# Where a second query projection stands in the opening of an encoder-layer kernel, and the order of its loads

## The chip, the cores and the metric

The kernel runs on one core of one Trainium2 chip. The metric is the device time of one execution in microseconds (us); a comparison uses the median of several runs. TensorE is PE in the profile (PEld its weight loads), VectorE is DVE, ScalarE is ACT, GpSimd is POOL, and SP is the engine that here only issues transfers. An "SPq" row is a transfer being issued by SP.

## The reference

One layer of a bidirectional encoder, on 1024 tokens of width 1024, in float32. The part that the change touches is the beginning:

```
mod = silu(c) @ w_ada + b_ada;  sh1, sc1, ... = split(mod, 6)
h   = rms_norm(x, norm_mix_g) * (1 + sc1) + sh1
q_a, k_a, v_a, qk_m, v_m, o_m, gates = split(h @ w_in)
y_attn = axial_gqa_attention(rope(rms_norm(q_a)), rope(rms_norm(k_a)), v_a)   # 8 heads, 2 kv heads
y_mem  = bidirectional_mlstm(silu(conv(qk_m)), v_m, o_m, gates)               # 4 heads
x = x + g1 * (concat(y_attn, y_mem) @ w_out)
... then the same norm and modulation, a SwiGLU feed-forward, a last norm
```

Two facts about it matter. The norm's root is one number per token and sc1, norm_mix_g are one number per channel, so h = (x * gain) * root + sh1, with gain = norm_mix_g * (1 + sc1). And so h @ w = ((x * gain) @ w) * root + sh1 @ w: a projection can be made on the *scaled* input z = x * gain before the root is known, and be mended afterwards with the root (per token) and with the shift row sh1 @ w (per output channel).

## The kernel before

Channels lie on the 128 partitions (eight tiles k of x, each 128 x 1024 tokens) and tokens along them, in two halves n of 512. To keep float32 accuracy, every operand of a matmul is split into a high part (a rounding to the PE's format, on ACT) and a low part (the rest, on DVE or POOL), and a product is three matmuls, `mm3` (L311): high by high, low by high, high by low. `hh`, `hl` are the two parts of the input, `whi`, `wlo` those of a weight piece (256 KB, from a raw buffer `wst`, of which there are three; six buffers for the split ones).

The whole program is laid out at build time by a small clock, `Clock` (L127): chains of steps are run in the order in which a model of the engines' durations says that they become ready, and instructions are emitted in that order. The engines then run in the order so written, each in sequence, and wait on semaphores. SP's queue is such a sequence too: a transfer whose buffer isn't free holds all that stand behind it.

The opening goes like this.
- `loads` (L590) lists the first transfers: `x0` to `x7`, `a8` to `a15` (rows of w_ada for the gain), `w` (raw weight pieces), then `a0` to `a7` (rows for the shift). Modulation rows (`ada`) are 512 KB and use five buffers; the dot with silu(c) on DVE frees each.
- For every k, `z_steps` makes the split scaled input from x and the gain, `square_steps` the squares for the norm. TensorE runs, for each k, three first units on it (key pair, value pair, first query unit, in `acc0`), for both halves: 18 matmuls of 512 columns for each k. After k = 5 the sums of squares are closed (L720) and `rstd_steps` makes the root. At k = 3 three `load_piece` calls split the next pieces; a piece's raw transfer is issued only when its own `load_piece` comes.
- `h_steps` (L686) then makes the normalized input in the same buffers as the scaled one: DVE multiplies x by the root, ACT applies gain and shift, ACT makes the high part, POOL the low one (DVE for the very first). The DVE step waits until TensorE has read the scaled input of this k (`z_read`).
- Behind that stand, on the normalized input, the chunk unit ("t", 0) (values of the memory heads and the gates, eight token blocks of 272 columns, tag `acct`) and the second query unit ("q", 1): for the first half of the tokens woven into the same loop over k, for the second half after the chunk unit's second half. `chunk_out` evicts each block into a staging buffer `vstg` (three of them) and stores it.
- `shift_sums` (L631) multiplies the shift into the weights that were used on the scaled input (`wagain`, loaded again by `load_again`, three of 512 KB); `rope_steps` and `v_steps` take the accumulators, multiply by the root (`rooted`), add the shift row (`shifted`) and go on with norm and rotation. For the second query unit `rooted` is a plain ACT copy.
- Then units from the list `IN` (third and fourth query, convolutions, chunks) run until the fourth query is rotated and the gates are ready, and attention starts (scores L1159, transposes L1191, values L1210), with the remaining units as filling between its matmuls.

Of the kernel before, what the change touches and what calls it, by code (L numbers as in the profile page):

```python
# [11 lines left out]
F32 = mybir.dt.float32  # L12
# [28 lines left out]
WARM = 34  # L41
PES = 3
# [43 lines left out]
class Engine:  # L86
# [5 lines left out]
    def __getattr__(self, op):  # L92
        fn = getattr(self.eng, op)

        def emit(*args, **kw):
            n = max(math.prod(a.shape[1:]) for a in args if hasattr(a, "shape"))
            self.clock.run(self.name, self.cost(op, n, args, kw))
            return fn(*args, **kw)  # L98
        return emit
# [27 lines left out]
class Clock:  # L127


    def __init__(self):  # L130
        self.t = self.now = self.fin = self.dma_t = self.dma_q = 0.0
        self.q = []
        self.n = 0
        self.free = {"act": 0.0, "dve": 0.0, "gps": 0.0}
        self.table = "exp"
        self.tick = None

    def run(self, eng, cost):
        e = self.free[eng] = max(self.free[eng], self.now) + cost
# [110 lines left out]
def layer_kernel(ctx, tc, xT, c, w_ada, vecs, cons, rope, w_f, w_fT, w_t0, w_t, w_o, w_gu, w_d, out):  # L250
# [114 lines left out]
    with tc.manual_schedule():  # L365
# [63 lines left out]
        start = {("t", 0): [6, 8, 9, 11], ("q", 1): [7, 10]}  # L429
        t0, q1 = chunk_w(0), conv_w(3)  # L430
        specs += [t0[0], q1[0], t0[1], t0[2], q1[1], t0[3]]
# [56 lines left out]
        def load_piece():  # L488
# [4 lines left out]
            while len(made) <= min(i + (AHEAD if i + AHEAD >= start["down"] else 0), len(specs) - 1):  # L493
# [3 lines left out]
            if isinstance(specs[i][0], str):  # L497
# [3 lines left out]
                  lo=dve if i >= start["down"] or i < 9 or start["o", 0] <= i < start["b", 1] else None)  # L501
# [21 lines left out]
        masks = stp.tile([P, 2 * P], F32, name="masks")  # L523
        nc.scalar.dma_start(masks, cons[:, P + 138:])
# [8 lines left out]
        sh2 = stp.tile([P, 3, 2], F32, name="sh2")  # L533
        shift = stp.tile([P, 3], F32, name="shift")
        shiftg = stp.tile([P, 3], F32, name="shiftg")
# [50 lines left out]
        for k in range(KT):  # L586
# [4 lines left out]
                 "x6", "x7", "a14", "a15", "a0", "a1", "a2", "a3", "a4", "a5", "a6", "a7"]  # L591

        def issue():
# [5 lines left out]
            elif kind == "a":  # L599
                ada_load(i)  # L600
            else:
# [29 lines left out]
        def shift_sums():  # L631
# [9 lines left out]
            def dot(f3, i):  # L641
                w = wagain[f3][:, halves(i)]
                dve.scalar_tensor_tensor(w, w, 1.0, rows[i][0], op0=OP.mult, op1=OP.mult, accum_out=sh2[:, f3, i:i + 1])
                if f3 == 2:
# [5 lines left out]
            def gains():  # L650
                for f3, n in ((0, "k_norm_g"), (2, "q_norm_g")):
# [17 lines left out]
        def load_again():  # L669

            for i in range(3):
# [10 lines left out]
        acc0 = [[psum_tile([P, HALF], "acc") for _ in range(NH)] for _ in range(3)]  # L682
# [17 lines left out]
        for k in range(KT):  # L700
            for n in range(NH):
                ck.need(z_ok[k][n])
                for f in range(3):
# [3 lines left out]
            if k < PES:  # L707
                for n in range(NH):
                    ck.need(sq_ok[k][n])
                    nc.tensor.matmul(msp[n][0], ones, by_pe[k, n], start=k == 0, stop=False)  # L710
                    ck.pe(0.86)
            z_read[k].set(ck, ck.t)
            if k == 3:
                for _ in range(3):
                    load_piece()
            if k == 5:
                for n in range(NH):
# [5 lines left out]
                    y_ok.append(ck.chain(0.0, rstd_ok[n], lambda n=n: act.activation(msp[n][0], rstd[n], AF.Copy)))  # L723
                for n in range(NH):
# [11 lines left out]
        def rope_steps(i, accs, raw=None, qg=None, more=FREE):  # L736
# [18 lines left out]
            def rooted(n):  # L755
                if raw < 0:
                    act.activation(qg[:, halves(n)], accs[n][0], AF.Copy)
                else:
                    dve.tensor_mul(qg[:, halves(n)], accs[n][0], rstd[n])
                accs[n][1].set(ck, ck.fin + LAT)  # L760

            def shifted():
                room()
                act.activation(X["sq"], qg, AF.Square, bias=shift[:, raw:raw + 1] if raw >= 0 else 0.0)
                act.activation(qg, qg, AF.Identity, scale=g, bias=shiftg[:, raw:raw + 1] if raw >= 0 else 0.0)
# [52 lines left out]
            else:  # L818
                ck.chain(0.0, rstd_ok[0], lambda: rooted(0), rstd_ok[1], more, lambda: rooted(1), shift_ok,
# [3 lines left out]
        def v_steps(accs):  # L823
            vt = bp.tile([P, S], F32, tag="big", name="vt")
# [98 lines left out]
        def chunk_out(ci, j, acc, f):  # L923
# [3 lines left out]
            stg = bp.tile([P, 2, P], F32, tag="vstg", name="vstg", bufs=3)  # L927
# [1193 lines left out]
        rope_steps(4, acc0[0], 0, raw_q[2])  # L2121
        rope_steps(0, acc0[2], 2, raw_q[0])
        for _ in range(3):
            load_piece()
        ck.chain(0.0, *sh_ok, load_again)
        ck.chain(0.0, y_free, load_tables)
        accs, tiles = [], []
        for n in range(NH):
            for j in range(4):
                ck.need(slot("acct").flag())  # L2130
                tiles.append(psum_tile([P, 272], "acct"))
            if n == 0:
# [209 lines left out]
```

## Time and profile before

| | us |
|---|---|
| runs, median (lowest, highest) of 3 | 1352.85 (1349.62, 1353.93) |
| the profiled execution | 1348.1 |
| its span | 1346.3 |
| PE / DVE / ACT / POOL busy in it | 1275.8 / 1053.4 / 709.6 / 537.6 |
| first matmul on the scaled input, last one | 11.6, 52.1 |
| first matmul on the normalized input | 57.0 |
| first scores of attention | 168.3 |

The profile is of one execution. A row of a timeline gives the start, the duration, the engine, the line, the operation with the tiles it writes and reads, how often, and in brackets how long the engine had stood idle before it and what released it. Every operation of DVE, ACT and POOL bears L98, the helper that emits them, so tiles tell them apart. A row of the busy table gives a stretch, its length, the busy time of PE, PEld, DVE, ACT and POOL with their instructions, the granted TensorE clock (1.00 is full), the DMA share and GB/s.

### The profile page before, as it was taken

The numbers are of one execution on the slowest core, as the hardware profiler recorded it, in microseconds if no ns is written. First come the engines' busy times: TensorE is split into PE (matmuls) and PEld (weight loads), VectorE is DVE, ScalarE is ACT, GpSimd is POOL, SyncE is SP. The second block draws the span as 40 slices with busy tenths as digits, with TensorE's granted clock in tenths as the row PEclk, the third lists the DMA queues.
The fourth block names the chain that finished last, engine by engine and source line by source line (L and its number), as shares of the span: only waits on it lengthen the run. The fifth ranks groups of instructions, "written<-read, shape, count | busy, mean of one in ns | idle before, by whom it ended". The sixth has DMA issues, their size and how long they took to land.

```text
span 1346.3 us, 19691 instructions
## 1 busy us (share of the span) xinstructions
PE 1275.8 (95%) x6656; PEld 1076.8 (80%) x6656; DVE 1053.4 (78%) x1683; ACT 709.6 (53%) x1342; POOL 537.6 (40%) x454
## 2 busy tenths in 40 slices
PE   9898888899999989999999999999999999999997
PEld 7687677888788988788778788888888887788886
DVE  6946699976689847989888989876666656888886
ACT  6575466778577855555477522333332334454462
POOL 0262578655666523444225155554544530000002
PEclk9898999999999999999999999999999999999999
DMA  9454433333233226673553344423332248933314
GB/s 362 139 154 134 115 104 100 86 103 109 67 93 107 74 82 193 218 271 114 181 173 116 108 143 144 138 94 110 111 117 78 80 170 314 340 106 94 94 56 164
DMA packets 104469, 187.04 MB, mean 139 GB/s; under 512 B 11568, under 2 KB 33200, under 8 KB 104368
## 3 DMA queue, kind: packets, MB, share of 16 engines
q1 hardware_dynamic: 90976, 163.68, 37.7%
q10 hardware_dynamic: 13392, 22.10, 4.3%
q8 instruction: 53, 0.87, 0.3%
q14 instruction: 48, 0.39, 0.1%
HBM read 139.33 MB, written 42.73 MB: 135 GB/s over the span
## 4 chain that ended last, share of the span: by engine, by line
PE 62%; DVE 20%; DMA 6%; ACT 5%; issue 4%; POOL 2%; SPq 1%; ACTq 0%; DVEq 0%; POOLq 0%
PE acc L312 17%; PE acc L314 17%; PE acc L313 17%; DVE sst L98 3%; DVE x L98 3%; DVE y L98 3%; DVE PT L98 2%; PE av L1210 2%; PE T L1191 2%; DVE ada L98 1%; PE S L1159 1%; DMA wst<-act_d 1%; ACT P L98 1%; DVE wlo L98 1%; PE ni L2001 1%
## 5 line engine op out<-in xcount | busy, mean ns | idle before, releaser
L98 ACT ACTIVATE whi<-wst 128x512 fp32r<-128x512 f32 (+2 forms) x223 | 134.0, 606 | 145.0 <-PE acc L314 61.0
L98 POOL TENSOR_TENSOR wlo<-wst,whi 128x512 fp32r<-128x512 f32 (+1 forms) x83 | 130.1, 1573 | 174.8 <-ACT whi L98 126.2
L313 PE MATMUL acc<-x,whi 128*128 128x512 f32 x352 | 136.9, 389 | 0.0
L98 POOL TENSOR_SCALAR P<-P,sst 128x1024 f32<-128x1024 f32 x64 | 85.9, 1343 | 85.5 <-DVE sst L98 64.2
L98 DVE TENSOR_TENSOR wlo<-wst,whi 128x512 fp32r<-128x512 f32 (+2 forms) x140 | 92.3, 663 | 30.6 <-ACT whi L98 30.1
L312 PE MATMUL acc<-hh,whi 128*128 128x512 f32 x224 | 96.3, 430 | 8.4 <-ACT xp L98 6.4
L98 POOL TENSOR_TENSOR x<-x,ny 128x256 f32<-128x256 f32 (+1 forms) x8 | 8.3, 1068 | 232.3 <-PE acc L314 212.3
L98 POOL TENSOR_TENSOR wlo<-wr,whi 128x512 fp32r<-128x512 f32 x52 | 72.3, 1389 | 71.5 <-ACT whi L98 68.4
L314 PE MATMUL acc<-whi,wcl 128*128 128x512 f32 x244 | 95.3, 390 | 2.2 <-DVE wcl L98 2.2
L312 PE MATMUL acc<-whi,wch 128*128 128x512 f32 x244 | 95.0, 390 | 1.2 <-ACT wch L98 1.2
L313 PE MATMUL acc<-wlo,wch 128*128 128x512 f32 x244 | 95.0, 389 | 0.0
L98 ACT ACTIVATE P<-S,sst,colq 128x1024 f32<-128x1024 f32 x64 | 77.2, 1206 | 31.9 <-DVE sst L98 26.9
L98 DVE TENSOR_TENSOR PT<-T,PT 128x512 fp32r<-128x512 f32 x128 | 83.4, 681 | 9.4 <-ACT PT L98 9.2
L313 PE MATMUL acc<-hl,whi 128*128 128x512 f32 x224 | 89.6, 400 | 0.3 <-DVE hl L98 0.3
L314 PE MATMUL acc<-hh,wlo 128*128 128x512 f32 x224 | 89.3, 399 | 0.1
L98 ACT ACTIVATE whi<-wr 128x512 fp32r<-128x512 f32 x56 | 35.3, 632 | 99.1 <-DVE wr L98 48.3
L312 PE MATMUL acct<-whi,hh 128*128 128x256 f32 (+1 forms) x256 | 81.4, 318 | 5.8 <-ACT hh L98 4.5
L98 ACT ACTIVATE PT<-T 128x512 fp32r<-128x512 f32 x128 | 71.7, 595 | 27.7 <-PE T L1191 26.9
L98 DVE TENSOR_REDUCE sst<-S 128x1 f32<-128x1024 f32 x64 | 77.6, 1213 | 7.6 <-PE S L1159 7.5
L1191 PE MATMUL T<-ident,P 128*128 128x128 f32 x512 | 71.2, 276 | 12.9 <-DVE PT L98 10.0
L98 POOL TENSOR_TENSOR ada<-ada,cond 128x512 f32<-128x512 f32 x48 | 72.2, 1507 | 20.5 <-DMA ada<-in_w_ada_dram 20.2
L1210 PE MATMUL av<-PT,va 128*128 128x256 f32 x512 | 71.9, 287 | 7.0 <-DVE PT L98 6.8
(482 smaller groups left out, 3851.3 us busy)
## 6 DMA issues: line engine op xcount, KB each, us to landing
wr<-in_w_gu_dram SPq DMA_DIRECT2D x66, 256.0 KB, 2.7
ada<-in_w_ada_dram SPq DMA_DIRECT2D x64, 256.0 KB, 3.4
wd<-in_w_d_dram SPq DMA_DIRECT2D x22, 512.0 KB, 6.6
wst<-in_w_gu_dram SPq DMA_DIRECT2D x42, 256.0 KB, 3.0
wst<-act_d SPq DMA_DIRECT2D x33, 256.0 KB, 3.6
ada<-in_w_ada_dram SPq DMA_DIRECT2D x16, 512.0 KB, 7.4
wst<-in_w_o_dram SPq DMA_DIRECT2D x32, 256.0 KB, 3.2
act_d<-sg ACTq DMA_DIRECT2D x29, 256.0 KB, 2.0
```

The lines of the kernel that those rows point to most:

```text
L98: return fn(*args, **kw)
L312: nc.tensor.matmul(acc, w[0], x[0], start=first, stop=False)
L313: nc.tensor.matmul(acc, w[0], x[1], start=False, stop=False)
L314: nc.tensor.matmul(acc, w[1], x[0], start=False, stop=last)
L1159: nc.tensor.matmul(sp[:, halves(n)], qs[:, j * P:(j + 1) * P], k2[g][m][:, halves(n)], start=m == 0, stop=m == 1)
L1191: nc.tensor.transpose(tp[:, k], Pt[q][:, (4 * b + k) * P:(4 * b + k + 1) * P], ident)
L1210: nc.tensor.matmul(av, va[:, k, h // 4], PT[it][m][:, k], start=(k, m) == (0, 0), stop=(k, m) == (NJ - 1, 1))
L2001: nc.tensor.matmul(ni, x["q"][:, i * P:(i + 1) * P], H["Cs"][b][:, i4], start=True, stop=True)
```

## The change

The second query unit moves from the normalized input to the scaled one and stands ahead of the chunk unit. The third of the first units (first query) is multiplied in two parts: k < `TAIL` in the common loop, the rest behind it. The root's sums are closed inside step k = `SUMS`. The query's correction then needs a fourth shift row. `h_steps` does gain and root in one DVE step, which no longer waits for `z_read`, and only the writing of the parts does; for three steps the parts are made straight from x by ACT and DVE. In `loads`, raw transfers `r` of six pieces stand ahead of and among a0 to a7, and in `load_piece` raw transfers run two pieces ahead for the third and fourth query and the first conv unit. The low parts of pieces 9 to 11 go from POOL to DVE. The masks are loaded at the end of the opening, by SP into another tile, instead of at the start by ACT. The last block of each half of the chunk unit has a staging buffer of its own. The value tile takes the place of the row of squares. The planner's clock now keeps DVE and POOL apart, in its model alone, where both have two inputs in SBUF, until attention starts.

```diff
+TAIL = 4
+SUMS = 6
...
+        if two and self.lock and eng in self.two:
+            other = "gps" if eng == "dve" else "dve"
+            s = max([s] + [b for a, b in self.two[other] if a <= s < b])
+            self.two[eng] = self.two[eng][-7:] + [(s, s + cost)]
...
-        start = {("t", 0): [6, 8, 9, 11], ("q", 1): [7, 10]}
+        start = {("t", 0): [8, 9, 10, 11], ("q", 1): [6, 7]}
...
-            while len(made) <= min(i + (AHEAD if i + AHEAD >= start["down"] else 0), len(specs) - 1):
+            while len(made) <= min(i + (AHEAD if i + AHEAD >= start["down"] or start["q", 2] <= i < start["f", 4] else 0), len(specs) - 1):
...
-                  lo=dve if i >= start["down"] or i < 9 or start["o", 0] <= i < start["b", 1] else None)
+                  lo=dve if i >= start["down"] or i < 12 or start["o", 0] <= i < start["b", 1] else None)
...
-        masks = stp.tile([P, 2 * P], F32, name="masks")
-        nc.scalar.dma_start(masks, cons[:, P + 138:])
...
-                 "x6", "x7", "a14", "a15", "a0", "a1", "a2", "a3", "a4", "a5", "a6", "a7"]
+                 "x6", "x7", "a14", "a15", "r", "r", "r", "a0", "a1", "a2", "a3", "a4", "r", "r", "r", "a5", "a6", "a7"]
...
+            elif kind == "r":
+                piece(len(made))
...
-            dots = [ck.chain(LAT, again[f3], lambda f3=f3: [dot(f3, i) for i in range(2)]) for f3 in range(3)]
+            dots = [ck.chain(LAT, again[f3], h_mul[4 + f3], lambda f3=f3: [dot(f3, i) for i in range(2)]) for f3 in range(4)]
...
+            def scaled():
+                dve.scalar_tensor_tensor(xs, xs, sc1[:, k:k + 1], rstd[n] if k < 2 else msp[n][0],
+                                         op0=OP.mult, op1=OP.mult)
+                if n:
+                    h_mul[k].set(ck, ck.fin)
...
-                0.0, *after, (rstd_ok if k < 2 else y_ok)[n], z_read[k],
-                lambda: dve.tensor_mul(xs, xs, rstd[n] if k < 2 else msp[n][0]), sh_ok[k],
-                lambda: act.activation(xs, xs, AF.Identity, scale=sc1[:, k:k + 1], bias=mod[:, k:k + 1]),
-                lambda: act.activation(h_hi[k][:, halves(n)], xs, AF.Copy),
-                lambda: (gps if n or k else dve).tensor_sub(h_lo[k][:, halves(n)], xs, h_hi[k][:, halves(n)].bitcast(F32)))
+                0.0, *after, (rstd_ok if k < 2 else y_ok)[n],
+                scaled, sh_ok[k], z_read[k],
+                *([lambda: act.activation(h_hi[k][:, halves(n)], xs, AF.Identity, bias=mod[:, k:k + 1]),
+                   lambda: dve.scalar_tensor_tensor(h_lo[k][:, halves(n)], xs, mod[:, k:k + 1],
+                                                    h_hi[k][:, halves(n)].bitcast(F32), op0=OP.add, op1=OP.subtract)]
+                  if n == 0 and k < 3 else
+                  [lambda: act.activation(xs, xs, AF.Identity, bias=mod[:, k:k + 1]),
+                   lambda: act.activation(h_hi[k][:, halves(n)], xs, AF.Copy),
+                   lambda: gps.tensor_sub(h_lo[k][:, halves(n)], xs, h_hi[k][:, halves(n)].bitcast(F32))]))
...
-                for f in range(3):
+                for f in range(3 if k < TAIL else 2):
...
-            stg = bp.tile([P, 2, P], F32, tag="vstg", name="vstg", bufs=3)
+            stg = (stp.tile([P, 2, P], F32, tag="vst0", name="vstg", bufs=1) if ci == 0 and j % 4 == 3 else
+                   bp.tile([P, 2, P], F32, tag="vstg", name="vstg", bufs=3))
...
+        for n in range(NH):
+            for k in range(TAIL, KT):
+                mm3(acc0[2][n][0], weights([2, 5], k, 4), (h_hi[k][:, halves(n)], h_lo[k][:, halves(n)]),
+                    k == 0, k == KT - 1)
+                ck.pe(0.68)
         rope_steps(0, acc0[2], 2, raw_q[0])
...
+        for k in range(KT):
+            for n in range(NH):
+                if k == 0:
+                    ck.need(slot("acc").flag())
+                    accs.append(psum_tile([P, HALF], "acc"))
                 mm3(accs[n][0], weights(start["q", 1], k, 4), (h_hi[k][:, halves(n)], h_lo[k][:, halves(n)]),
                     k == 0, k == KT - 1)
                 ck.pe(0.68)
+            z_read[k].set(ck, ck.t)
+            if k == 1:
+                for _ in range(3):
+                    load_piece()
+        rope_steps(1, accs, 3, raw_q[1])
```

After that the chunk unit stands alone: for each half, k = 0 to 5 over its four blocks, and then k = 6 and 7 block by block, each evicted as it ends; between them six more `load_piece` calls. `shift_sums` follows the first half as before.

More of the change, by code (lines that the diff above doesn't have):

```diff
@@ L96, in emit @@
             n = max(math.prod(a.shape[1:]) for a in args if hasattr(a, "shape"))
-            self.clock.run(self.name, self.cost(op, n, args, kw))
+            ins = [a for a in args[1:] if hasattr(a, "shape") and math.prod(a.shape[1:]) > 8]
+            self.clock.run(self.name, self.cost(op, n, args, kw),
+                           len(ins) == 2 and all(getattr(a, "space", None) != PSUM for a in ins))
             return fn(*args, **kw)
@@ L669, in load_again @@
         def load_again():
-            for i in range(3):
+            for i in range(4):
                 w = wagain[i] = bp.tile([P, S], F32, tag="big", name="wagain")
@@ L680, in load_tables @@
             ck.chain(arrive, lambda: None, flag=rp_ok)
-        acc0 = [[psum_tile([P, HALF], "acc") for _ in range(NH)] for _ in range(3)]
+        acc0 = [[None] * NH for _ in range(3)]
+        for f, n in ((0, 0), (1, 0), (0, 1), (1, 1), (2, 0), (2, 1)):
+            acc0[f][n] = psum_tile([P, HALF], "acc")
+        h_mul = [Flag() for _ in range(KT)]
         for _ in range(WARM):
@@ L706, in layer_kernel @@
                     ck.pe(0.68)
[L707 to L717, printed above, removed]
+                if k == SUMS:
                     ck.need(sq_ok[7][n])
@@ L723, in layer_kernel @@
                     y_ok.append(ck.chain(0.0, rstd_ok[n], lambda n=n: act.activation(msp[n][0], rstd[n], AF.Copy)))
+            if k < PES:
+                for n in range(NH):
+                    ck.need(sq_ok[k][n])
+                    nc.tensor.matmul(msp[n][0], ones, by_pe[k, n], start=k == 0, stop=False)
+                    ck.pe(0.86)
+            if k == 3:
+                for _ in range(3):
+                    load_piece()
+            if k == SUMS:
                 for n in range(NH):
@@ L734, in layer_kernel, with rope_steps @@
         va_ok = [Flag(), Flag()]
-        def rope_steps(i, accs, raw=None, qg=None, more=FREE):
+        def rope_steps(i, accs, raw=None, qg=None):
             is_k = i == 4
@@ L755, in rooted @@
             def rooted(n):
[L756 to L759, printed above, removed]
+                dve.tensor_mul(qg[:, halves(n)], accs[n][0], rstd[n])
                 accs[n][1].set(ck, ck.fin + LAT)
@@ L823, in v_steps @@
         def v_steps(accs):
-            vt = bp.tile([P, S], F32, tag="big", name="vt")
+            vt = ssx_t
             def transpose(b):
@@ L2145, in query, with chunk_step @@
                 ck.pe(0.68)
-            for k in range(KT):
-                ck.need(h_ok[n][k])
-                chunk_step(k)
-                if n == 0:
-                    query(k)
-                elif k % 2:
-                    load_piece()
-            for j in range(4 * n, 4 * n + 4):
-                chunk_out(0, j, *tiles[j])
+            z_read[k].set(ck, ck.t)
+            if k == 1:
+                for _ in range(3):
+                    load_piece()
+        rope_steps(1, accs, 3, raw_q[1])
+        ck.chain(0.0, *sh_ok, load_again)
+        ck.chain(0.0, y_free, load_tables)
+        for n in range(NH):
+            def chunk_step(j, k):
+                ck.need(h_ok[n][k])
+                if k == 0:
+                    ck.need(slot("acct").flag())
+                    tiles.append(psum_tile([P, 272], "acct"))
+                s = slice(j * P, (j + 1) * P)
+                mm3(tiles[j][0], (h_hi[k][:, s], h_lo[k][:, s]), weights(start["t", 0], k, 2), k == 0, k == KT - 1)
+                ck.pe(0.38)
+                if k == KT - 1:
+                    chunk_out(0, j, *tiles[j])
+            js = range(4 * n, 4 * n + 4)
+            for k in range(KT - 2):
+                for j in js:
+                    chunk_step(j, k)
+                if k % 2 and (n or k < 4):
+                    load_piece()
+            for j in js:
+                for k in range(KT - 2, KT):
+                    chunk_step(j, k)
+            if n:
+                load_piece()
             if n == 0:
-                more = Flag()
-                rope_steps(1, accs, -1, raw_q[1], more)
                 while not again:
@@ L2163, in layer_kernel @@
                 ck.chain(0.0, *vo_ok[0], gate_steps)
-                ck.need(slot("acc").flag())
-                accs.append(psum_tile([P, HALF], "acc"))
-                for k in range(KT):
-                    query(k)
-                    if k % 4 == 3:
-                        load_piece()
-                more.set(ck, ck.t)
+        masks = small()
+        maskin = dma(masks[:, 0:2 * P], cons[:, P + 138:])
         for e in range(2):
             for i in range(2):
-                ck.at(1.0, lambda e=e, i=i: dve.tensor_copy(maskb[:, e, i], masks[:, e * P:(e + 1) * P]))
+                ck.at(maskin, lambda e=e, i=i: dve.tensor_copy(maskb[:, e, i], masks[:, e * P:(e + 1) * P]))
         un = Stream(units(IN))
```

46 lines of the change are left out of this document (17 added, 29 removed).

## The prediction

> **What bounds the kernel now.** I read the page first, for the share of each engine, then busy time by stretches of the opening, then TensorE's waits, then the timeline of each engine around the two long ones.
>
> ```profile
> span 1346.3 us, 19691 instructions
> PE 1275.8 (95%) x6656; PEld 1076.8 (80%) x6656; DVE 1053.4 (78%) x1683; ACT 709.6 (53%) x1342; POOL 537.6 (40%) x454
> ```
>
> TensorE is busy 95% of the span, so only 70 us in the whole kernel are not matmul. Where they lie decides. Busy time by stretches (busy microseconds of PE, PEld, DVE, ACT, POOL, then the granted TensorE clock):
>
> ```profile
> 50.00:60.00 10.00, 4.81 (x19) 3.72 (x19) 10.00 (x17) 7.68 (x14) 1.78 (x2) 0.85 0.40 133
> 60.00:70.00 10.00, 8.76 (x49) 8.00 (x48) 10.00 (x13) 5.33 (x10) 10.00 (x6) 0.81 0.28 71
> 100.00:110.00 10.00, 6.24 (x18) 4.04 (x17) 6.10 (x8) 3.70 (x8) 3.49 (x2) 0.73 0.40 123
> 110.00:120.00 10.00, 10.00 (x51) 8.39 (x50) 9.38 (x17) 4.83 (x8) 2.69 (x2) 0.92 0.27 88
> 52.30:111.70 59.40, 47.93 (x273) 41.14 (x273) 38.89 (x67) 40.82 (x76) 33.72 (x23) 0.89 0.39 117
> ```
>
> The last row is the stretch that the change rewrites: from the last matmul on the scaled input to the first of the third query unit. Idle there is 59.4 - 47.9 = 11.5 us; the clock lost is 59.4 x (1 - 0.89) = 6.5 us. Together **18.0 us** in which TensorE does less than it could. TensorE's waits up to 150 us name the idle part (total, times, longest):
>
> ```profile
> PE acct L312 <- ACT hh L98: 4.5, 1, 4.5
> PE ms L777 <- DVE sq L98: 3.8, 1, 3.8
> PE acct L314 <- POOL hl L98: 2.1, 2, 1.2
> PE acct L314 <- DVE hl L98: 0.7, 1, 0.7
> PE acct L312 <- ACT vstg L98: 0.4, 1, 0.4
> ```
>
> The first is the hole between the last matmul on the scaled input (52.1 us) and the first on the normalized one; the second comes some 50 us later. Both are followed by a granted clock under 1. The timelines of PE, SP, ACT and DVE say why:
>
> ```profile
> 52.10 0.39 PE L314 MATMUL acc<-hh,wlo 128*128 128x512 f32 x1
> 56.97 0.59 PE L312 MATMUL acct<-whi,hh 128*128 128x272 f32 x1 [4.49 <-ACT hh L98]
> ...
> 22.45 20.75 SPq L317 DMA_DIRECT2D ada<-in_w_ada_dram  x8
> 43.28 0.38 SPq L317 DMA_DIRECT2D wst<-in_w_t_dram  x1
> ...
> 47.36 0.66 ACT L98 ACTIVATE whi<-wst 128x544 fp32r<-128x544 f32 x1 [3.05 <-DMA wst<-in_w_t_dram]
> 47.92 0.67 ACT L98 ACTIVATE sq<-ms,both 128x512 f32<-128x512 f32 x1
> ...
> 52.96 1.29 DVE L98 SCALAR_TENSOR_TENSOR sq<-sq 128x512 f32<-128x512 f32 x2
> ...
> 102.91 0.38 ACT L98 ACTIVATE vstg<-acct 128x256 f32<-128x256 f32 x1 [5.40 <-DMA v_d<-vstg]
> 103.19 0.68 ACT L98 ACTIVATE sq<-ms,both 128x512 f32<-128x512 f32 x1
> 106.46 2.08 PE L777 MATMUL ms<-sqk,con 128*128 128x512 f32 x2 [3.76 <-DVE sq L98]
> ```
>
> First hole: SP issues in order and is held by the modulation loads until 43.2, so the first raw piece of the chunk unit leaves at 43.28; ScalarE, in order too, stands 3.05 us before its split and only then (47.92) starts the root of the mean square, which VectorE ends at 54.2. Second hole: ScalarE waits 5.40 us for a staging buffer whose store is not done, and the root of the key norm is queued behind.
>
> **The change, part by part.** Matmul work is the same: the two query halves, the chunk unit and the three first units have as many products as before. So I lay them out anew at the durations of these rows.
>
> ```profile
> 34.05 0.39 PE L314 MATMUL acc<-hh,wlo 128*128 128x512 f32 x1
> 34.27 0.39 PE L312 MATMUL acc<-hh,whi 128*128 128x512 f32 x1
> ...
> 42.44 1.88 PE L720 MATMUL ms<-ssx,ones 128*128 128x512 f32 x4
> 43.76 0.80 PE L312 MATMUL acc<-hh,whi 128*128 128x512 f32 x1
> ...
> 92.66 0.29 PE L312 MATMUL acct<-whi,hh 128*128 128x272 f32 x1
> 92.79 0.29 PE L313 MATMUL acct<-wlo,hh 128*128 128x272 f32 x1
> ```
>
> A 512-column product starts 0.227 us after the one before it (34.05 to 34.27, about), a 272-column one 0.125. Steps k = 4 to 7 lose the third unit: 12 products, 2.72 us each instead of 4.09. From 34.3 on: k = 4, 5 to 39.7; k = 6 with the two closing sums of squares inside (1.32 us by the 42.44 row, and 0.8 for the switches) to 44.5; k = 7 to 47.3; the tail, 24 products, to 52.7; the second query unit, 48, to 63.6; the chunk unit 2 x 96 x 0.125 = 24.0, the two row sums 1.4, transposes and norm sums some 4.5 (an estimate: a bit over two of the 1.88 of the 42.44 row), so the third query unit could start at 93.5 instead of 111.7. **Ceiling: 18.2 us**, which agrees with the 18.0 above, reached the other way.
>
> Can the inputs follow this? DVE is the one to watch:
>
> ```profile
> 39.68 1.41 DVE L98 SCALAR_TENSOR_TENSOR hl<-x,sc,hh 128x512 fp32r<-128x512 f32 x2
> ...
> 20.00:30.00 10.00, 10.00 (x40) 7.06 (x38) 9.51 (x18) 7.17 (x12) 0.00 (x0) 1.00 1.03 418
> 41.70:89.00 47.30, 39.60 (x212) 33.32 (x212) 37.64 (x65) 33.54 (x68) 24.98 (x17) 0.93 0.41 130
> ...
> 61.95 1.28 DVE L98 SCALAR_TENSOR_TENSOR ada<-ada,cond 128x1024 f32<-128x1024 f32 x1
> 63.16 2.30 DVE L98 SCALAR_TENSOR_TENSOR ada<-ada,cond 128x1024 f32<-128x1024 f32 x1
> ...
> 60.79 5.88 POOL L98 TENSOR_TENSOR wlo<-wst,whi 128x544 fp32r<-128x544 f32 x3
> 66.64 5.73 POOL L98 TENSOR_TENSOR hl<-x,hh 128x512 fp32r<-128x512 f32 x3
> ```
>
> Scaled input: its last step is split at 41.1, and step 7 is needed at 44.5. Even if the three splits of pieces 6 to 8 (0.66 each on DVE), whose raw loads now stand ahead of the modulation's, come in front, 1.4 us are left: no stall. Root: the last add of squares follows that split, the sums close on TensorE between 42 and 44.5, and ScalarE no longer waits for a late weight; the old chain took 47.9 to 54.2 = 6.3 us, so the roots are there by 50 or 51. The second query unit needs two sum banks back at 52.7, after two or three products of 0.68 us on DVE: on time, with about a microsecond to spare. It covers the first hole.
>
> What is added. DVE: two more low parts of the normalized input (ScalarE saves three copies, POOL two subtractions), three low parts of weights taken from POOL, two evacuations by the root that were ScalarE copies, two more products for the fourth shift row. That is 9 operations of about 0.69 us, 6.2 us on the 37.6 that DVE has in the same 47.3 us: 43.8, hidden but only just. SP: one more load of 512 KB for the shift row, and the masks at the end of the opening rather than the start; neither has a matmul waiting. The six raw loads ahead of and among a0 to a7 cost their time on a full DMA: three of 256 KB at the 418 GB/s of the window from 20 to 30 us make a0 to a4 some 1.9 us later; a5 to a7 wait behind pieces 9 to 11, and these for the splits of 6 to 8, done around 43; but the eighth of the old modulation loads in the SP row left only at 43.2. Their shifts are needed by the chunk unit at 63.6 + 5 x 1.5 = 71, so I take nothing.
>
> New stalls. The normalized input of step k can be written only after the query unit has read the scaled one, so from 54 on in steps of 1.4 us; then ScalarE (two operations, about 1.3) and POOL (1.3 alone, 1.9 by the 66.64 row) carry it. 13 POOL steps of 1.9 are 25 us, from about 58 to 83, and TensorE wants the last near 86. Bounds from the waits: between 0 and 2 x (2.1 + 0.7 + 0.4) = 6.4 us; I take **4**, above the middle, because DVE comes so near to full. A gain from this part is excluded, since it adds waits only.
>
> *Shared access.* Of two modulation products in a row, both beside POOL's subtractions (rows of 61.95, 63.16 and 60.79), one lasts 1.28 us and the next 2.30. [...] In rows: if all nine double as that product did, the 43.8 become 50.0, which is 2.7 us more than there are. This is part of the first rival below.
>
> The staging buffer: a fourth one for each half of the chunk unit, so the fourth eviction doesn't wait for a store. The 5.40 us of ScalarE go, and with them the second hole of 3.76 us and its clock; what is late next is the rotary product on DVE, which no matmul waits for. Raw weights two pieces ahead for the third and fourth query and the first conv units: SP issues them before the stores that hold it; the waits listed up to 150 us hold none for such a weight, so 0.
>
> Sum to the third query unit: 18.2 - 4 = **14 us**.
>
> **Does it reach the end?**
>
> ```profile
> 170.00:200.00 30.00, 26.20 (x143) 21.88 (x141) 29.26 (x37) 19.73 (x37) 21.29 (x12) 0.94 0.34 104
> 320.00:350.00 30.00, 29.26 (x174) 24.75 (x173) 19.23 (x32) 21.26 (x46) 20.14 (x17) 1.00 0.26 76
> 100.00:160.00 60.00, 53.19 (x247) 42.94 (x245) 40.62 (x48) 27.81 (x44) 21.24 (x15) 0.94 0.44 130
> 168.29 1.98 PE L1159 MATMUL S<-k,qs 128*128 128x512 f32 x8
> 166.56 1.68 DVE L98 SCALAR_TENSOR_TENSOR y<-xp,y 128x1024 f32<-128x1024 f32 x1 [5.09 <-ACT xp L98]
> ```
>
> The first scores are at 168.3. From there VectorE is full (29.3 of 30), later TensorE is (29.3 of 30); both only slide. Between the opening and the scores no engine is full (DVE 40.6 of 60). So most passes on; I keep 13 of 14 for the new order that the planner's clock gives to what follows. The profiled execution took 1348.1 us (span 1346.3 and 1.8 around it): 1348.1 - 13 = 1335. The median of the runs, 1352.85, lies 4.75 above it, and by the same gain it becomes **1340**.
>
> **Rivals.** *The normalized input sets the pace.* If ScalarE, POOL and the fuller VectorE can't follow, the chunk unit waits: the stalls double to 8 and bring a clock dip like the 3.5 us of 100 to 120 (10 x 0.27 + 10 x 0.08): 18.2 - 8 - 3.5 = 6.7, of which 6 pass on: 1347. For it: DVE at 43.8 of 47.3. Against: steps of 1.4 us on TensorE are longer than each engine's share.
>
> *The gain ends at the scores.* They wait for key, third and fourth query rotation, a chain of stores and loads. If that chain starts no earlier, nothing but filling is gained: 1352, no change. For it: DVE and SP work between 112 and 168 in series. Against: the shift rows come earlier too, since the row sums stand right behind the first half of the chunk unit.
>
> *Slower: convolutions slide into the full stretch.* The first conv unit's last VectorE step ends at 168.2, just as the scores begin. If the earlier scores leave two such units, each with six full-width operations, for the stretch where VectorE is full, each costs 6 x 1.68 = 10 us; 20 against the 14 is +6: 1359. It decides when the scores start before the first conv unit's silu and the second's too.
>
> *It doesn't do what it says:* the query unit still waits, because the roots come late on VectorE; then the hole of 4.5 us is only moved ahead of it, and with the staging buffer alone 7 us are left (3.76 + 3.5), of which 6.5 pass on: 1346.
>
> **How the numbers follow.** Forecast 0.58, pace 0.16, hole only moved 0.06, gain ends at the scores 0.10, slower 0.10. A difference under 0.3%, 4 us, can't be told from none. The forecast's own range is the ceiling of 18 and up to 6 more where later stalls go too, 1329, to 8 us, 1345. Up to 1352 the range takes in the pace and most of the no-change case; the slower ones lie beyond. Faster: 0.58 + 0.06 + 0.10 of the pace, 0.74; within 0.3%: 0.06 of the pace and 0.09 of the scores' case, 0.15; slower 0.11.
>
> **What would show it.** Right: no idle of over 1 us between the last product on the scaled input and the chunk unit, granted clock 1.00 from 50 to 110, the first root on ScalarE near 43, the third query unit near 97, first scores near 155. Wrong: TensorE waiting for hl by POOL for more than 6 us, or for a VectorE evacuation at the query unit; first scores still near 168; or a stretch after the scores in which VectorE is full for longer than before.

## The result, and the profile after

The changed kernel takes 1383.14 us (median of 4 runs, 1379.95 to 1389.2) where the kernel before, on the same chip, takes 1353.37: a ratio of **1.0234 [1.0203, 1.0264]**. It is 2.3% slower; 1340 was forecast. The profiled execution took 1379.95 us, its span is 31.8 us longer than before. From here "after" is the changed kernel.

The page of after, first lines:

```profile
span 1378.1 us, 19717 instructions
PE 1283.3 (93%) x6656; PEld 1081.2 (78%) x6656; DVE 1060.6 (77%) x1694; ACT 706.7 (51%) x1338; POOL 517.8 (38%) x449
```

The matmuls are the same in number. PE is busy 7.5 us longer (its mean granted clock is 0.976, in before 0.988) and idle 24.3 us longer (94.8 against 70.5). Busy time of after by stretches, columns as before:

```profile
50.00:60.00 10.00, 10.00 (x46) 8.28 (x45) 9.96 (x18) 5.17 (x11) 0.00 (x0) 1.00 0.36 125
60.00:70.00 10.00, 10.00 (x69) 9.41 (x68) 10.00 (x17) 7.57 (x18) 3.06 (x3) 1.00 0.78 282
100.00:110.00 10.00, 9.11 (x39) 6.84 (x38) 7.64 (x14) 2.19 (x5) 2.21 (x2) 0.83 0.39 91
110.00:120.00 10.00, 6.18 (x35) 4.77 (x33) 6.82 (x14) 3.86 (x9) 1.34 (x3) 0.90 0.21 62
120.00:130.00 10.00, 10.00 (x40) 8.72 (x40) 6.83 (x13) 0.90 (x3) 0.00 (x0) 0.59 0.60 177
500.00:550.00 50.00, 23.98 (x182) 22.34 (x180) 18.57 (x49) 15.55 (x35) 14.91 (x28) 0.78 0.60 192
```

The hole of 50 to 60 is gone, at full clock. But 110 to 130 has become worse, and a stretch of which the prediction says nothing stands half empty: 500 to 550. The same stretch of before:

```profile
500.00:550.00 50.00, 45.36 (x297) 41.04 (x298) 34.80 (x102) 29.70 (x77) 22.97 (x44) 0.93 0.70 216
```

**The opening came out better than forecast.** The timeline of after, ACT's root, the two waits inside the chunk unit, and the first product of the third query unit:

```profile
42.26 0.69 ACT L102 ACTIVATE sq<-ms,both 128x512 f32<-128x512 f32 x1 [1.91 <-PE ms L735]
...
74.25 0.39 PE L325 MATMUL acct<-whi,hl 128*128 128x272 f32 x1 [1.01 <-POOL hl L102]
...
89.29 0.39 PE L325 MATMUL acct<-whi,hl 128*128 128x272 f32 x1 [0.98 <-POOL hl L102]
...
92.64 0.39 PE L323 MATMUL acc<-hh,whi 128*128 128x512 f32 x1
```

The third query unit starts at 92.64, where 97 was forecast, and some 19 us sooner than in before (111.89).

**Then 100 to 130 gave it back.** The timeline of after goes on:

```profile
101.13 1.10 PE L798 MATMUL ms<-sqk,con 128*128 128x512 f32 x2 [0.80 <-PE acc L325]
102.32 1.92 PE L805 MATMUL ms<-con,sqk 128*128 128x2 f32 x16
104.09 0.55 PE L323 MATMUL acc<-hh,whi 128*128 128x512 f32 x1
104.44 0.63 PE L324 MATMUL acc<-hl,whi 128*128 128x512 f32 x1
...
113.31 1.84 PE L805 MATMUL ms<-con,sqk 128*128 128x2 f32 x16
...
115.18 0.69 ACT L102 ACTIVATE qg<-acc,vec 128x512 f32<-128x512 f32 x1 [9.29 <-PE ms L805]
...
119.93 3.57 PE L805 MATMUL ms<-con,sqk 128*128 128x2 f32 x16 [3.82 <-DVE rqv L102]
123.36 0.77 PE L323 MATMUL acc<-hh,whi 128*128 128x512 f32 x1
...
169.95 3.78 PE L1181 MATMUL S<-k,qs 128*128 128x512 f32 x8 [3.50 <-POOL qs L102]
```

The norm sums of the key (L798) and of the first three query units (L805) share two banks of PSUM (the memory that matmuls write to), the "aux" ring, and each bank comes free only when DVE and ACT have made the root out of it. Now that the second query unit is early, its sum stands in that queue with the key's, the first's and the third's. ACT, in order, stands 9.29 us, until the norm sum of 113.31 is done, before it evicts the third query unit; PE then waits 3.82 us for a bank, and the clock falls to 0.59. The first scores come at 169.95, where they were at 168.29.

**And the largest loss lies between attention and the memory heads.** PE's waits of after from 450 to 620 us, the longest:

```profile
PE tr L1911 <- DVE W L102: 27.6, 2, 25.6
```

The chain of waits of after names what DVE does meanwhile (start, length, what):

```profile
522.82 2.84 DMA ada<-in_w_ada_dram
...
527.55 3.50 DMA ada<-in_w_ada_dram
...
534.94 0.71 DVE ada L102 x2
535.67 2.91 DMA ada<-in_w_ada_dram
538.68 0.71 DVE ada L102 x2
539.40 2.63 DMA ada<-in_w_ada_dram
...
549.20 0.70 DVE ada L102 x2
...
550.18 0.68 DVE W L102 x2
551.00 0.66 PE tr L1911 x2
```

They belong to the last 16 half rows of the modulation (256 KB each, for its sixth vector, the feed-forward's gate g2). They have two buffers, so two are loaded, multiplied on DVE, and only then the next two can be loaded: in the whole chain 2.6 to 3.5 us of transfer and 0.7 of DVE a pair, with next to nothing beside them. The memory heads' product W stands behind them on DVE, though it does not use them, and PE's transposition waits for W.

Why are they alone? The loop that runs the memory heads and the filling together can put such a row in at every step that it writes out. But it ends as soon as the filling is used up; behind it stands a loop that writes out whatever rows are left, in a row:

```
ck.tick = lambda: all(f.done for f in heads[0]["in"]) and ada_late(64)
ck.streams(mem, [un], stop=lambda: un.wait is None and all(f.done for v in vo_ok for f in v))
while not summed:
    ck.need(*adas[-2:])
    ada_late(64)
```

There are 768 chunk products (matmuls of a chunk unit) in all; 192 of them are the opening's own chunk unit, the rest is filling. In PE's instruction order as it is written out, before has done 588 of the 768 ahead of the first memory-head transposition, after has done 726. SP's row of after says the same from the other side, twelve rows issued as one run that lasts 19.63 us:

```profile
526.95 19.63 SPq L328 DMA_DIRECT2D ada<-in_w_ada_dram  x12
```

In before no more than two such rows stand in a run there, the longest of them:

```profile
513.23 4.16 SPq L317 DMA_DIRECT2D ada<-in_w_ada_dram  x2
```

**The sum.** A chunk product takes 0.12 us (the pieces of the chain of waits). The last values of attention end at 493.6 in before (491.44 + 2.12) and at 504.3 in after (502.19 + 2.08), 10.7 us later; but by then, with all other products the same in number, after has done 660 chunk products and before 552, which is 108 x 0.12 = 13.0 us of work that before still has to do. So after is 2.3 us *ahead* at the end of attention, all that is left of some 19. From there to the end of the span it takes 873.8 us and before 852.7, with 13.0 us less to do: 34.1 us lost, and 34.1 - 2.3 = 31.8.

### The profile page after: what moved, and what is told of

It is laid out like the page before. It is cut to its first block, busy times and chain, and to the rows that moved or that the text cites. A ratio compares the mean times of both kernels' runs of the same rounds, so it can differ in the third digit from the quotient of the medians.

```text
span 1378.1 us, 19717 instructions
## 1 busy us (share of the span) xinstructions
PE 1283.3 (93%) x6656; PEld 1081.2 (78%) x6656; DVE 1060.6 (77%) x1694; ACT 706.7 (51%) x1338; POOL 517.8 (38%) x449
## 4 chain that ended last, share of the span: by engine, by line
PE 63%; DVE 18%; DMA 6%; issue 5%; ACT 4%; POOL 2%; SPq 0%; ACTq 0%; DVEq 0%; POOLq 0%
PE acc L325 16%; PE acc L324 16%; PE acc L323 16%; DVE sst L102 3%; DVE y L102 3%; PE av L1232 2%; DVE x L102 2%; DVE PT L102 2%; PE T L1213 2%; PE S L1181 2%; DMA ada<-in_w_ada_dram 2%; DVE ada L102 1%; POOL hl L102 1%; PE ni L2023 1%; PE acct L323 1%
## 5 line engine op out<-in xcount | busy, mean ns | idle before, releaser
L102 POOL TENSOR_TENSOR wlo<-wst,whi 128x512 fp32r<-128x512 f32 x80 | 119.5, 1501 | 162.0 <-ACT whi L102 103.8
L102 DVE TENSOR_TENSOR wlo<-wst,whi 128x512 fp32r<-128x512 f32 (+2 forms) x143 | 95.8, 675 | 31.7 <-ACT whi L102 31.1
L102 POOL TENSOR_SCALAR P<-P,sst 128x1024 f32<-128x1024 f32 x64 | 80.8, 1263 | 100.1 <-DVE sst L102 71.6
L102 DVE TENSOR_TENSOR PT<-T,PT 128x512 fp32r<-128x512 f32 x128 | 83.9, 682 | 18.3 <-ACT PT L102 18.2
L102 ACT ACTIVATE PT<-T 128x512 fp32r<-128x512 f32 x128 | 72.3, 597 | 20.6 <-PE T L1213 19.6
L323 PE MATMUL acct<-whi,hh 128*128 128x256 f32 (+1 forms) x256 | 77.7, 304 | 1.2 <-ACT vstg L102 1.1
```

The lines of the kernel that those rows point to most:

```text
L323: nc.tensor.matmul(acc, w[0], x[0], start=first, stop=False)
```

## The experiments

Theory A: the change uses nearly all of the filling up before the memory heads begin, and the modulation rows, which need the filling beside them, then stand alone. Theory B: the new opening itself, its loads and its order, makes everything later, wherever the wait shows. Ratios are always to the kernel before on the same chip.

**The loop goes on until the rows are done** (after_rows). Only the end condition changes, so that the memory heads' steps go on between the rows:

```diff
-        ck.streams(mem, [un], stop=lambda: un.wait is None and all(f.done for v in vo_ok for f in v))
+        ck.streams(mem, [un], stop=lambda: un.wait is None and all(f.done for v in vo_ok for f in v) and summed)
```

> The changed kernel, in which the loop that leads from attention to the memory heads no longer ends when the filling units are used up but only when the last 16 modulation rows are through too, so that they are written between the steps of the memory heads instead of twelve in a row ahead of them. Theory A (the change runs out of filling matmuls before the memory heads begin, and the remaining rows then stand alone on VectorE with TensorE idle 25.6 us): the 25.6 us and some of the lower clock after it go: 1383 becomes 1355 to 1363. Theory B (the new opening itself makes everything behind it later, and the idle time there would only show up elsewhere): 1375 or more.

Measured: 1358.14 us, ratio 1.0065 [1.0049, 1.0082]. The wait of the transposition, in PE's waits of this kernel:

```profile
PE tr L1911 <- DVE W L102: 5.2, 1, 5.2
```

27.6 us have become 5.2, and the ratio falls by 1.7%, about 23 us. The opening is untouched, first scores at 168.28. That is A, for some 23 of the 31.8 us.

**The kernel before, robbed of its filling** (before_spent): the units that are left are run to their end ahead of the memory heads, with nothing else changed.

```diff
+        ck.streams([un])
         mem = [Stream(g) for g in (ends(), backs(), fronts(), all_states())]
```

> The kernel before, its opening untouched, but with the remaining filling units run to their end ahead of the first step of the memory heads, so that nothing is left beside the modulation rows. Theory A: fourteen rows stand in a row on VectorE, at about 1.85 us each TensorE idles some 25 us more, and the kernel before becomes as slow as the changed one: 1353 becomes 1376 to 1386. Theory B: the place of the filling matters little, since the matmuls are the same: 1350 to 1362.

Measured: 1396.51 us, ratio 1.0348 [1.0325, 1.0371]: the same loss without any of the change, and more of it. PE's waits of this kernel there, and SP's row:

```profile
PE tr L1889 <- DVE W L98: 25.0, 1, 25.0
PE acct L312 <- ACT whi L98: 8.1, 1, 8.1
```

```profile
538.25 23.18 SPq L317 DMA_DIRECT2D ada<-in_w_ada_dram  x14
```

The wait for W is that of after, nearly to the microsecond. The 8.1 us beside it are the filling running on its own, waiting for its weights. The time lies 10.5 us above theory A's bounds; that these 8.1 us are most of the excess is argued, no run takes them apart.

**The query units' norm sums in the six banks** (after_slots): three places, tag "acc" for "ms" where it isn't the key.

```diff
-                    ms, f = psum_tile([P, NJ, 2], "ms")
+                    ms, f = psum_tile([P, NJ, 2], "acc")
...
-                         *[(slot("ms"), lambda n=n: squares(n)) for n in range(NH if is_k else 1)])
+                         *[(slot("ms" if is_k else "acc"), lambda n=n: squares(n)) for n in range(NH if is_k else 1)])
```

> The changed kernel, in which the norm sums of the query units (16 small matmuls each) write to the ring of six accumulators instead of the two auxiliary banks that they share with the key's norm, the value transposes and the gates. Theory A: the third query's norm no longer waits 3.8 us in TensorE's queue between third and fourth query unit, the fourth unit starts some 8 us earlier (idle and clock from 115 to 130), and with less filling used up by the end of attention the row of modulation rows at the transition is shorter, 6 instead of 12: 1383 becomes 1360 to 1370. Theory B: the order of the norms is not what delays the fourth query unit: 1378 to 1388.

Measured: 1356.3 us, ratio 1.0046 [1.0031, 1.0061], a little below theory A's bounds. In the busy table 120 to 130 is at full clock, and the timeline has the first scores 14.3 us sooner than after:

```profile
120.00:130.00 10.00, 10.00 (x49) 8.28 (x48) 4.82 (x5) 2.10 (x3) 0.00 (x0) 1.00 0.80 227
```

```profile
155.65 2.11 PE L1181 MATMUL S<-k,qs 128*128 128x512 f32 x8 [1.87 <-POOL qs L102]
```

So it was the queue on the two banks that kept the gain from the scores. The edit also moved the written order: 654 chunk products are spent at the transposition instead of 726, and the longest run of rows is 6.

**Both repairs** (after_both), the two edits above together.

> The changed kernel with both edits: norm sums of the queries in the accumulator ring, and the transition that waits for the modulation rows too. Theory A: the 18 us that the opening gains by the third query unit are then kept in part: 1338 to 1352. Theory B: 1370 or more.

Measured: 1340.75 us, ratio 0.9940 [0.9922, 0.9958], faster than both kernels. First scores at 155.33, span 1336.9. The wait for W, in PE's waits:

```profile
PE tr L1911 <- DVE W L102: 4.0, 2, 3.0
```

**Is that the repairs' gain alone?** (before_both): both edits in the kernel before.

> Control: the kernel before with both repairs (norm sums of the query units in the ring of six banks; the first memory-head loop kept on until the modulation rows are summed), without the change. The order written out has the same filling left at the transition as before (588 chunk products spent before the first memory-head transposition in both) and the modulation rows spread in the same way (2, 4, 2, 2, 2, 4 ahead of the first seven products W). Theory A (the gain of the doubly repaired kernel is the change's own, once it is neither queued on two banks nor left without filling): this kernel takes the time of before, ratio 0.998 to 1.003, 1347 to 1354 us. Rival R (the two repairs are a gain by themselves, the change adds nothing): ratio near 0.994, 1340 to 1344 us.

Measured: 1348.62 us, ratio 0.9979 [0.9962, 0.9995]: within 0.3% of before, as A has it. The intervals nearly touch, so both kernels were run once more side by side.

> The kernel before with both repairs, once more, now on the same chip as the changed kernel with both repairs, so that the two can be compared directly. Earlier: 0.9979 [0.9962, 0.9995] of the kernel before. Theory A: 0.996 to 1.000, 4 to 6 us above the changed kernel with both repairs. Rival R (the gain is the repairs' alone): within 2 us of the changed kernel with both repairs.

> The changed kernel with both repairs, once more, on the same chip as the kernel before with both repairs. Earlier: 0.9940 [0.9922, 0.9958] of the kernel before. Theory A: 0.992 to 0.996, so the change itself is worth 4 to 6 us once the filling and the banks are seen to. Rival R: 0.996 to 1.000, the same as the kernel before with both repairs.

Measured: 1349.41 us without the change, ratio 0.9994 [0.9981, 1.0007], and 1342.23 us with it, ratio 0.9935 [0.9918, 0.9951]. On one chip the change is worth 7.2 us once the two repairs are in, where 4 to 6 were expected; the repairs alone are worth nothing that can be told.

**The planner's new rule left out** (after_nolock). The instructions of the opening stay, only the order that the planner's clock gives differs.

```diff
-        self.lock = True
+        self.lock = False
```

> The changed kernel with the planner's new rule for VectorE and GpSimd (two-operand work on one delays the other in the planner's clock) left out from the start. Nothing of the instructions or loads of the opening is removed; only the order that the clock gives. By the order written out, 633 chunk products are spent at the first memory-head transposition (588 before, 726 after), and the modulation rows are spread 3, 4, 2, 2, 5 ahead of the products W (after: 16 in a row ahead of the second). Theory A (filling spent early leaves the rows alone): most of the loss goes, 1354 to 1364 us, ratio 1.003 to 1.010, the wait of the transposition for W under 8 us. Theory B (the new opening itself, its loads and moved query unit, costs the time): no change against the changed kernel, 1378 to 1386 us, ratio 1.020 to 1.026.

Measured: 1355.41 us, within theory A's bounds, and ratio 1.0021 [0.9998, 1.0044], just below them: most of the loss is gone. First scores come at 154.87, with all norm sums on the same two banks as in after, and the wait for W is 2.6 us. So neither the loads nor the moved unit has to cost time; B falls here as well. With the banks as they are, the order decides whether they are a queue. Another wait has become the longest behind attention, in a memory head's later transposition:

```profile
549.54 1.53 PE L2087 MATMUL tr<-ident,hs 128*128 128x128 f32 x4 [9.68 <-DVE hs L102]
```

The same wait is 7.4 us in after_slots, and no more than 1.2 at a time in after_both, which differs from after_slots by the end of the loop alone: there it goes with the bare loop. It may be much of what lies between 1.0021 here and 0.9940 in after_both; no run takes that apart.

**Raw loads two pieces ahead left out** (after_noahead):

```diff
-            while len(made) <= min(i + (AHEAD if i + AHEAD >= start["down"] or start["q", 2] <= i < start["f", 4] else 0), len(specs) - 1):
+            while len(made) <= min(i + (AHEAD if i + AHEAD >= start["down"] else 0), len(specs) - 1):
```

> The changed kernel with the third part of the change undone: raw weights of the units of the filling are no longer loaded two pieces ahead. By the order written out all 768 chunk products are spent at the first memory-head transposition, and all 16 modulation rows stand in a row ahead of the first product W. Theory A: as slow as the changed kernel or slower, 1380 to 1395 us, ratio 1.022 to 1.033. Theory C (the raw loads two pieces ahead take the DMA engines and buffers and so cost the time): faster than the changed kernel, 1350 to 1370 us, ratio 1.000 to 1.015.

Measured: 1396.51 us, ratio 1.0337 [1.0312, 1.0363]: slower than after, as A has it, and slightly beyond A's bounds. PE's wait for W there is 21.3 us, and SP's timeline shows fifteen rows in a run:

```profile
PE na L2018 <- DVE W L102: 21.3, 1, 21.3
```

```profile
530.57 25.00 SPq L328 DMA_DIRECT2D ada<-in_w_ada_dram  x15
```

**The same two parts, and the loads, on the repaired kernel** (both_nolock, both_noahead, both_rlate). The last takes all six "r" out of `loads`, so that these weights stand behind the modulation rows again.

> The doubly repaired changed kernel without the planner's new rule. Order written out: 654 chunk products at the first memory-head transposition and rows 3, 3, 3, 1, 2, 4, both the same as with the rule. Theory A: within 3 us of the doubly repaired kernel, 1338 to 1344 us, ratio 0.992 to 0.997. Theory B (the rule keeps work off a contended pair of engines and so is worth some us of its own): 1346 to 1354 us, ratio 0.998 to 1.003.

> The doubly repaired changed kernel with the third part undone: raw weights of the filling's units are not loaded two pieces ahead. Order written out: 654 chunk products at the first memory-head transposition and rows 3, 3, 3, 1, 2, 4, both as with the loads ahead. Theory A (in the changed kernel this part acted through what was left of the filling, which here is the same): within 3 us of the doubly repaired kernel, 1338 to 1345 us, ratio 0.992 to 0.997. Rival (loading two pieces ahead is worth its own time, whatever the order): 1347 to 1356 us, ratio 0.999 to 1.005.

> The doubly repaired changed kernel with the second part of the change undone: the raw weights of the second query unit and of the first chunk unit are no longer issued ahead of the eight modulation loads, but behind them, when the unit is prepared. From the trace of the doubly repaired kernel: the raw weights of the second query unit are issued at 22.24 to 24.77 us there, and the last of the modulation loads ahead of which they stand is issued at about 45 to 47 us; the unit's products begin about 47 us. Behind the modulation loads they land at about 49 to 51 us, and the rounding and the difference follow on ACT and DVE. Order of the filling and of the modulation rows later on: as with the loads ahead (654 chunk products at the first memory-head transposition; 3, 3, 3, 1, 2, 4). Theory A (the moved unit needs the loads ahead): TensorE stands 3 to 8 us near 50 us at a wait for whi or wlo, 1343 to 1350 us, ratio 0.995 to 1.000. Rival (the loads ahead are worth nothing): no wait over 1 us there, 1338 to 1343 us, ratio 0.991 to 0.996.

Measured: 1345.47 us, 0.9960 [0.9946, 0.9975]; 1343.67 us, 0.9948 [0.9931, 0.9966]; 1345.13 us, 0.9963 [0.9949, 0.9978]. All three intervals overlap with that of the doubly repaired kernel, so none of the three parts can be told from nothing there. With the loads late, PE does wait near 50 us, though less than was expected and by way of a sum bank that DVE frees late (PE's waits):

```profile
PE acc L323 <- DVE ssx L102: 2.1, 1, 2.1
```

Its first scores come 2.8 us later than in after_both (158.14 against 155.33). In the other two they come at 160.90 without the planner's rule, though the total time can't be told apart, and at 153.09 without the loads ahead. After_rows and after, whose openings are the same, differ by 1.7 us at this mark. Both_rlate is inconclusive, with a lean to theory A; of the other two, both_noahead lies within A's bounds, and both_nolock does so by its ratio but not by its microseconds.

**Spent filling and runs of rows, side by side.** Spent: chunk products of 768 ahead of the first memory-head transposition, in the written order. Run: rows that SP issues in one run there, and how long it lasts.

| kernel | spent | longest run | ratio |
|---|---|---|---|
| before | 588 | 2 | 1 |
| before, both repairs | 588 | 2 | 0.9979, 0.9994 |
| after, no planner rule | 633 | 3 (6.4 us) | 1.0021 |
| after, both repairs | 654 | 3 (7.4 us) | 0.9940, 0.9935 |
| after, both repairs, less one part (three kernels) | 654 | 3 (6.3 to 7.4 us) | 0.9960, 0.9948, 0.9963 |
| after, norm sums moved | 654 | 6 (9.8 us) | 1.0046 |
| after, loop goes on | 726 | 2 | 1.0065 |
| after | 726 | 12 (19.6 us) | 1.0234 |
| before, filling spent | 768 | 14 (23.2 us) | 1.0348 |
| after, not two ahead | 768 | 15 (25.0 us) | 1.0337 |

The three slowest kernels are those with a run of twelve or more. Filling spent early is not itself the loss (726 with runs of two is 1.0065); what it uncovers is. Among the other kernels neither column gives the order.

## Why the prediction was wrong

*What bounds the kernel; the two holes.* Right. 11.5 us of idle and the clock of 0.89 were there, and up to the third query unit the change removed nearly all of it: 2.0 us of idle are left from 52.3 to 92.64, at full clock. But a hole like the second one came back behind that, the 3.82 us at L805.

*Ceiling 18.2 us, third query unit from 111.7 to 93.5, less 4 of stalls.* The moves are right, the stalls too large: the chunk unit's waits for hl are 2.0 us, and the unit starts at 92.64, sooner than even the ceiling. Part of that is luck: of the 4.5 us that the sum took for transposes and norm sums ahead of the unit, only the transposes stand there (1.04 us at 89.52); the norm sums come behind its start, from 101.13 on, and so are work put off. VectorE, from 41.7 to 89, came to 40.5 us, not to the 43.8 of the sum:

```profile
41.70:89.00 47.30, 45.60 (x271) 39.89 (x269) 40.50 (x74) 33.54 (x67) 22.06 (x17) 1.00 0.43 141
```

The prediction's 50.0 us, with all nine added operations slowed as one modulation product was beside POOL (2.30 us, the one before it 1.28), was the author's estimate from that one product. In before three of the four modulation products beside POOL's operations take 2.27 to 2.38 us, and no run isolates what slows them; in after VectorE as a whole has 6.8 of the 47.3 us to spare. So such slowing did not set the pace here, and the rival built on it is out.

*"What is late next is the rotary product on DVE, which no matmul waits for."* Wrong. What is late next are the norm sums, and matmuls are what waits: 3.82 us at L805, behind two banks. The prediction had counted who waits for the staging buffer, but not how many users the aux ring would have once four norms come close together. Moving the sums to the ring of six brought the scores from 169.95 to 155.65, the "near 155" that was forecast.

*Raw weights two pieces ahead: "so 0".* As a transfer, yes (0.9948 beside 0.9940 on the repaired kernel). As a change of the written order, no: leaving it out of after moves 42 more products ahead of the transposition, and the ratio from 1.0234 to 1.0337.

*"So most passes on; I keep 13 of 14 for the new order that the planner's clock gives to what follows."* **This is the step that failed**, twice. Between the opening and the scores no engine was full (in before, from 100 to 160, PE is busy 53.2 of 60 us and DVE 40.6), and the prediction took that to mean that the gain slides through; the bank queue was not an engine. And behind the scores "both only slide" left out that the filling is a stock: with the same order of units, work done sooner is missing later. The stretch from 500 to 550 had no term at all: in before 216 chunk products, some 26 us, are still left when attention ends, and they lie beside the rows. The step took 1 us off for everything behind the third query unit. Measured, some 17 of the 19 us were gone by the end of attention, and 34.1 us were lost behind it. The doubly repaired kernel shows what the step was worth without the two. Its last values end at 483.2, 10.4 us sooner than in before, with 39 more chunk products done (591 against 552, 4.7 us): 15 us ahead, so the 14 was sound up to there. Of these, 9.4 reach the end of the span (1336.9 against 1346.3); the rest goes behind attention, where the filling is again shorter than in before, by 66 products at the transposition; that the one comes of the other is argued here, not shown.

*The rivals.* "The gain ends at the scores" was half right: its mark, first scores still near 168, came true, and the forecast's own list called it the sign of being wrong. But it priced what comes behind at nothing, 1352. The slower rival had the right sign and the wrong place: VectorE is not full for longer behind the scores (from 170 to 200 it is busy 25.4 of 30 us, in before 29.3). "The hole only moved" did not happen as described, since the moved query unit does not wait (PE has no idle time from 41 to 63.3, where it ends); the hole of 25.6 us that ends at 551.0 is another one.

What stays open: why the planner's clock hands attention more filling (from the first scores to the last values 732 products of both kinds against 651) is not shown, only that the count depends on each part of the order. Nor is it settled where the remaining 0.65% of after_rows lies; the norm queue is in it, since both repairs together take it away and 0.6% more.

## What to carry to other kernels

Filling is a stock, not a stream: before you value work done sooner, find the last place that lives on it, and look at what stands there if it runs out one step early. Wherever a plan ends a mixed loop on "nothing left to fill with", read what the bare loop behind it writes out, and give it an end condition of its own. And when an edit lets a step come earlier, count the users of every small ring that it then shares (two PSUM banks here), not only the busy time of the engines.

## What the runs showed of the hardware

PE was listed as busy and still lost its clock. In after, between the product that ends at 100.33 and the one that starts at 104.09, PE idles 0.80 us and else runs two 512-column products of one norm sum and sixteen products of 2 columns (rows of 1.10 and 1.92 us); behind them, 512-column products follow one another every 0.43 us from 104.44 to 107.82, at a granted clock of 0.51, against 0.23 at 1.00 from 107.82 on. In before the same sums with no idle time, 2.6 us from 97.14 to 99.70, left the clock at 1.00 up to 102.70. In before's second hole, where PE is idle from 102.70 to 106.46, the granted clock is at half from 104.70 on, 2.0 us into the hole:

```profile
102.70:104.70 2.00, 0.00 (x0) 0.00 (x0) 0.80 (x2) 1.20 (x4) 0.00 (x0) 1.00 0.20 69
104.70:106.46 1.76, 0.00 (x1) 0.00 (x1) 1.76 (x4) 1.69 (x4) 0.60 (x1) 0.50 0.47 149
```

How long PE has been idle when the clock halves is not the same in every hole. In after's wait of 3.82 us, from 116.11 to 119.93, the clock is at half from 118.11 on, again 2.0 us into the hole; but in before's first hole, where PE is idle from 52.49 to 56.97, it is still at 0.99 from 55.00 to 56.97 and at 0.50 only from there to 63.00. Nor is there always that much idle time ahead of it: in after only 0.80 us of the 3.76 from 100.33 to 104.09 are idle, and 3.38 us at half rate follow, from 104.44 to 107.82. The 0.59 of 120 to 130 is 0.50 up to 128.00, behind 3.82 us of waiting and with 3.57 us of products of 2 columns; whether such products bear on the clock at all, no run here shows.
